# Fixed shares of other work behind the steps of each attention block, in place of a weaver that looks at readiness

## The chip, the cores and the metric

The kernel runs on one core of a Trainium2 chip. The metric is the device time of one execution in microseconds (us), the median of three runs. The kernel before takes 1716.58 us (1715.23 to 1721.32).

## What is computed

One layer of a hybrid block on 1024 positions of width 1024 in float32: a normalisation, one wide projection, an mLSTM branch in two directions (4 heads), a differential attention branch (8 heads), two gated output projections that are added, a last projection and a normalisation. The change touches only the attention:

```python
def diff_attention(q, k, v, lam):            # 8 heads, blocks of 128 queries
    def one_block(qb):
        scores = jnp.einsum('bqhjd,bkhjd->bhjqk', qb, k) * scale      # j = 2 halves of a head
        p = jax.nn.softmax(scores, axis=-1)
        p_diff = p[:, :, 0] - lam * p[:, :, 1]
        return jnp.einsum('bhqk,bkhd->bqhd', p_diff, v)
```

Queries and keys pass through a rotation by position (rope) first; the result of a head is normalised over its 128 columns and multiplied by a gate.

## The kernel before

Every float32 product is made of three matmuls on operands split into a high and a low part (`wH`, `wL`, `pH`, `pL`, and so on). The program is a list of units, each with a planned cost, and TensorE executes them in exactly the order of that list. The orders of the other engines come from a scheduler that puts each instruction where its own estimate of time finds it ready; at run time each engine then goes through its order strictly.

The attention has 8 heads of 8 blocks (t = 0 to 7, 128 queries each). `da_cycle` gives the units of one block:

- S: 12 matmuls into two PSUM tiles of two banks each. Behind it stand, off TensorE, per half a maximum on VectorE (line 963) and an exp on ScalarE (line 965), then three VectorE steps that give `e` = p0 - lam p1 (lines 969 to 971).
- T0 and T1: 4 transpositions each of the `e` of the block before, into one bank; then the casts `pH` (ScalarE, line 984) and `pL` (VectorE, line 985).
- P, in odd blocks: 24 matmuls (line 996) with the values of two earlier blocks; behind them a ScalarE copy `att` (line 998).
- M, in even blocks: 2 transpositions of `att` and two squares on ScalarE (line 1008), which write in the same bank. After the fourth M of a head (block 2 of the next head) eight small GpSimd steps (lines 145 to 151 and 1015) make a root.
- G, in blocks 4 and 5: 4 transpositions, and a VectorE step `zg` (line 1028) that reads them.

T, P, M and G share two PSUM banks (tag T): each of them needs a bank that an earlier one has given back. For T0 and T1 this is a bank of P (given back by the `att` copy), of M (by its second square) or of G (by the `zg` step); which of them is settled when the program is built.

Between these units stands other work, in pieces of three matmuls of 512 columns (line 460) or, for the values, six of 256 columns (line 482). In even heads these are the rope projection of the next head (pieces 1 to 32) and its gate z (33 to 48); in odd heads the rope projection (1 to 32) and the values of the next two heads (33 to 64); in the last head 32 pieces of gates for a later stage. The rope projection hands on a chain: two VectorE products from PSUM (lines 894 and 895), GpSimd `m` (896, 897), ScalarE casts `hl` (899), GpSimd remainders (900), DMAs to `kst` and `qq`. Its weights are cast on ScalarE (`wH`, line 193) and completed on GpSimd (`wL`, line 194).

The order of units and pieces is the work of `Weaver.weave`: it takes next the unit whose inputs and banks its plan holds to be ready soonest, and among equals the one that lies furthest behind in its share of the head. `z[h]` of odd heads are two loads without TensorE cost.

Of the kernel before, what the change touches and what calls it, by code (L numbers as in the profile page):

```python
# [13 lines left out]

S = 1024
D = 1024
# [3 lines left out]
L = 256  # L20
NC = S // L
NB = L // 128
# [6 lines left out]
def two_pi_parts():  # L29
# [9 lines left out]
MM = 0.214  # L39
TP = 0.109  # L40

LAG = dict(Th=2.2, Sh=5.0, PVh=3.7, Mh=8.1, qk=14.0, T=6.8, PV=3.7, M=4.5, F=6.0, TTh=1.9, TT=3.2, POh=1.6,
           PO=1.7, Wh=0.3, W=2.0, STh=2.1, ST=4.9, th=1.8, t=4.1, aq=9.0, outh=6.6, out=14.0, G=6.0)
# [18 lines left out]
class Weaver:  # L62
# [28 lines left out]
    def weave(self, *lists):  # L91


        lanes = {}
        for i, un in enumerate(lists):
            total, c = sum(u.cost for u in un) or 1.0, 0.0
            for u in un:
                lanes.setdefault((i, u.lane), []).append((c / total, u))
                c += u.cost
        self.coming = {u.name for un in lists for u in un if u.name}  # L100
        heads = list(lanes.values())
        while heads:
            best = min(heads, key=lambda l: (max(self.ready(l[0][1]), self.now), l[0][0]))
            u = best.pop(0)[1]
            self.put(u)
            self.coming.discard(u.name)
            heads = [l for l in heads if l]


class Block:  # L110
# [199 lines left out]
    def big(self, n, dt=F32):  # L310
        return self.s0.tile([128, S + 4], dt, name=n, tag="big", bufs=6)

# [61 lines left out]
    def conv_sink(self, seg, n):  # L374
# [3 lines left out]
        def sink(i, j, ps, rest):  # L378
            if i not in box:
                box[i] = (self.big("cin"), [])  # L380
                p.memset(box[i][0][:, 0:2], 0.0)
                p.memset(box[i][0][:, S + 2:S + 4], 0.0)
            raw, got = box[i]
# [9 lines left out]
            w = lambda j: self.conv[:, j * 16 + base:j * 16 + base + 1]  # L393
            y = self.big("y")[:, 0:S]
            for half in range(2):
# [247 lines left out]
    def angles(self, an):  # L643
# [38 lines left out]
        for src in (cs, sn):  # L682
            reps.append(self.big("rep")[:, 0:S].rearrange("p (k a b) -> p k a b", k=8, a=4))
            for k in (0, 4):
# [258 lines left out]
    def da_parts(self, h, st):  # L943
        v, a, p, q, w1 = self.v, self.a, self.p, self.q, self.w1

        def scores(t):
            if t == 0:
                st["Z"] = w1.tile([128, 2, 8], F32, name="Z", tag="Z", bufs=2)
                st["ms"] = w1.tile([128, 8], F32, name="ms", tag="ms", bufs=2)
                st["att"] = w1.tile([128, S], F32, name="att", tag="att", bufs=1)  # L950
            qq, k = st["q", t // 4], st["k"]
            c = slice((t % 4) * 128, (t % 4) * 128 + 128)
            Z = st["Z"]
            both = [self.bank("S", (128, S)) for _ in range(2)]

            for o in (slice(0, 512), slice(512, S)):
                for m, (x, y) in enumerate(((0, 0), (0, 1), (1, 0))):
                    for j, ps in enumerate(both):
                        r = slice(64 * j, 64 * j + 64)
                        self.t.matmul(ps[:, o], lhsT=qq[r, x, c], rhs=k[r, y, o], start=(m == 0), stop=(m == 2))  # L960
            for j, ps in enumerate(both):
                nm = w1.tile([128, 1], F32, name="nm", tag="nm", bufs=3)
                v.tensor_reduce(out=nm, in_=ps, axis=AX.X, op=ALU.max, negate=True)  # L963
                e = w1.tile([128, S], F32, name=f"e{j}", tag=f"e{j}", bufs=2 if j == 0 else 1)
                a.activation(out=e, in_=ps, func=AF.Exp, bias=nm[:, 0:1], accum_out=Z[:, j, t:t + 1])  # L965
                st["e", j] = e
            e0 = st["e", 0]
            r = w1.tile([128, 1], F32, name="r", tag="r", bufs=1)
            v.reciprocal(out=r, in_=Z[:, 1, t:t + 1])
            v.tensor_scalar(out=r, in0=r, scalar1=Z[:, 0, t:t + 1], scalar2=self.nlam[:, 0:1], op0=ALU.mult, op1=ALU.mult)  # L970
            v.scalar_tensor_tensor(out=e0, in0=e, scalar=r[:, 0:1], in1=e0, op0=ALU.mult, op1=ALU.add)
            st["p", t] = e0

        def transposes(t, g):
            pt = st["p", t]
            s = slice((t % 2) * 128, (t % 2) * 128 + 128)
            if t % 2 == 0:
                st["pT", t // 2, g] = (w1.tile([128, 4, 256], F32R, name="pH", tag="pH", bufs=2),
                                       w1.tile([128, 4, 256], F32R, name="pL", tag="pL", bufs=2))
            pH, pL = st["pT", t // 2, g]  # L980
            ps = self.bank("T", (128, 4, 128))
            for i in range(4):
                self.tr(ps[:, i, :], pt[:, (4 * g + i) * 128:(4 * g + i + 1) * 128])
            a.copy(pH[:, :, s], ps)  # L984
            v.tensor_tensor(out=pL[:, :, s], in0=ps, in1=pH[:, :, s].bitcast(F32), op=ALU.subtract)  # L985
# [14 lines left out]
        def squares(t2):  # L1000
            pt = self.bank("T")
            for i in range(2):
                t = 2 * t2 + i
                self.tr(pt[:, i * 128:(i + 1) * 128], st["att"][:, t * 128:(t + 1) * 128])
            for i in range(2):
                t = 2 * t2 + i
                x = pt[:, i * 128:(i + 1) * 128]
                a.activation(out=x, in_=x, func=AF.Square, accum_out=st["ms"][:, t:t + 1])
            if t2 == 3:
                zz = w1.tile([128, 8], F32, name="zz", tag="zz", bufs=1)  # L1010
                Z0 = st["Z"][:, 0, :]
                p.tensor_scalar(out=zz, in0=Z0, scalar1=EPS, scalar2=None, op0=ALU.mult)
                p.tensor_tensor(out=zz, in0=zz, in1=Z0, op=ALU.mult)
                rs = self.rsqrt(w1, st["ms"], 1.0 / 128.0, zz, "rb", eng=p)
                p.tensor_scalar(out=rs, in0=rs, scalar1=(1.0 - LAMBDA_INIT) * 0.5, scalar2=None, op0=ALU.mult)
                for half in range(2):
                    g = st["g", half]
                    p.tensor_tensor(out=g, in0=st["att"][:, half * 512:(half + 1) * 512], in1=g, op=ALU.mult)
                st["rs"] = rs

        def scale(half):
# [3 lines left out]
            for i in range(4):  # L1025
# [3 lines left out]
            q.dma_start(out=self.yb[h][:, half * 512:(half + 1) * 512], in_=g)  # L1029

        return dict(
            S=lambda t: Unit(6 * MM, lambda: scores(t), tag="S", hold=LAG["Sh"], name=("S", h, t), after=((("qk", h), LAG["qk"]),)),
            T=lambda t, g: Unit(4 * TP, lambda: transposes(t, g), tag="T", hold=LAG["Th"], name=("T", h, t, g),
                                after=((("S", h, t), LAG["T"]),)),
            PV=lambda t2, g: Unit(12 * TP, lambda: pv(t2, g), tag="T" if g == 0 else None, hold=LAG["PVh"], name=("PV", h, t2, g),
                                  after=((("T", h, 2 * t2 + 1, g), LAG["PV"]),)),
            M=lambda t2: Unit(2 * TP, lambda: squares(t2), tag="T", hold=LAG["Mh"], name=("M", h, t2),
                              after=((("PV", h, t2, 1), LAG["M"]), (("z", h if t2 == 3 else -1), 0.0))),
            G=lambda half: Unit(4 * TP, lambda: scale(half), tag="T", hold=LAG["Th"], name=("G", h, half),
                                after=((("M", h, 3), LAG["F"]),)))  # L1040
# [425 lines left out]
    def build(self):  # L1466
# [21 lines left out]
        with pool(name="const", bufs=1) as self.const, \  # L1488
# [22 lines left out]
            for n in range(NH_A):  # L1511
# [5 lines left out]
                if n < 3:  # L1517
                    blocks = (("gb", 4), ("gb", 5)) if n == 0 else (("bz", 4 * n - 3), ("bz", 4 * n - 1))
# [26 lines left out]
            w = Weaver()  # L1545
            w.add(enter("h", "hpool"), enter("tab", "tab", side="right"), enter("tf", "tf", side="right"),
                  enter("p0", "p0", side="right"), banks("ps0", T=6), keep(E.PE, E.Activation, E.DVE, E.Pool), do(begin))
            k = self.PIECES
# [30 lines left out]
            for i, x in enumerate(products + [None]):  # L1579
                y = products[i - 1] if i else None  # L1580
                un = sum(([x[0]] if x else []) + ([y[6]] if y else []) + ([x[3]] if x else []) + ([y[5]] if y else [])
                         + ([x[1], x[4], x[2]] if x else []), [])
# [5 lines left out]
            qk, z = zip(*[self.da_proj(h, sts[h]) for h in range(NH_B)])  # L1588
            w.add(do(lambda: setattr(self, "ahead", True)), *qk[0], *self.da_v(0, sts[0:2]))
            prev = None  # L1590
            for h in range(NH_B):
                cur = self.da_parts(h, sts[h])
                main = sum((self.da_cycle(cur, prev, t) for t in range(8)), [])
                ahead = qk[h + 1] if h + 1 < NH_B else []
                if h + 1 == NH_B:
                    nxt = fill(FILL[h])
                elif h % 2 == 1:
                    nxt = ahead + self.da_v((h + 1) // 2, sts[h + 1:h + 3])
                else:
                    nxt = ahead + z[h]  # L1600
                if h % 2 == 1:

                    k = [i for i, u in enumerate(main) if u.name and u.name[0] == "G"][-1] + 1
                    main[k:k] = z[h]
                w.weave(main, nxt)
                prev = cur
            end = sum((self.da_cycle(None, prev, t) for t in range(6)), [])
            w.weave(end[:-2], fill(2))
# [25 lines left out]
            k = len(passA) // 2  # L1634
# [52 lines left out]
```

## Time and profile before

| | |
|---|---|
| median of three runs | 1716.58 us |
| the profiled execution | 1714.09 us, span 1712.3 us |
| TensorE busy in the span | 1651.9 us (96%) |
| ScalarE, VectorE, GpSimd busy | 789.2, 1003.2, 630.7 us |
| granted TensorE clock, mean | 0.994 of full speed |
| attention, about 499 to 1105 us of the span | 606 us |

Busy time of TensorE is modelled, since matmuls overlap: a matmul of 256 columns is shown as 0.28 us long while the next one starts 0.12 us later. In the timeline the distance from start to start is therefore the price of an instruction, and an idle stretch costs somewhat more than its idle time.

### The profile page before, as it was taken

The numbers are of one execution on the slowest core, as the hardware profiler recorded it, in microseconds if no ns is written. First come the engines' busy times: TensorE is split into PE (matmuls) and PEld (weight loads), VectorE is DVE, ScalarE is ACT, GpSimd is POOL, SyncE is SP. The second block draws the span as 40 slices with busy tenths as digits, with TensorE's granted clock in tenths as the row PEclk, the third lists the DMA queues.
The fourth block names the chain that finished last, engine by engine and source line by source line (L and its number), as shares of the span: only waits on it lengthen the run. The fifth ranks groups of instructions, "written<-read, shape, count | busy, mean of one in ns | idle before, by whom it ended". The sixth has DMA issues, their size and how long they took to land. (4 is left out here: it accounts for less than half of the span.)

```text
span 1712.3 us, 25475 instructions
## 1 busy us (share of the span) xinstructions
PE 1651.9 (96%) x9395; PEld 1384.6 (81%) x9395; DVE 1003.2 (59%) x1817; ACT 789.2 (46%) x1578; POOL 630.7 (37%) x698
## 2 busy tenths in 40 slices
PE   7999999999999999999999999999999989999998
PEld 5777877888787897788779778789999877888887
DVE  5778586666538666766666566425666743235533
ACT  7455454544435554545454455324655644122221
POOL 5767566666534323241433332122321411222000
PEclk9999999999999999999999999999999999999999
DMA  5344343443443212222312131165454327344222
GB/s 183 94 128 128 107 129 117 135 148 111 124 99 75 49 51 62 74 69 56 83 33 70 50 87 50 56 184 164 140 167 155 93 85 254 122 147 136 87 88 85
DMA packets 177935, 182.99 MB, mean 107 GB/s; under 512 B 12441, under 2 KB 135666, under 8 KB 177810
## 3 DMA queue, kind: packets, MB, share of 16 engines
q1 hardware_dynamic: 176898, 179.78, 35.1%
q8 instruction: 74, 1.21, 0.3%
q10 hardware_dynamic: 912, 1.59, 0.2%
q14 instruction: 51, 0.42, 0.1%
HBM read 116.21 MB, written 48.33 MB: 96 GB/s over the span
## 5 line engine op out<-in xcount | busy, mean ns | idle before, releaser
L460 PE MATMUL pj<-hH,wH 128*128 128x512 f32 x544 | 227.7, 419 | 1.9 <-ACT f L573 1.5
L460 PE MATMUL pj<-hH,wL 128*128 128x512 f32 x544 | 214.3, 394 | 1.8 <-POOL wL L207 1.8
L460 PE MATMUL pj<-hL,wH 128*128 128x512 f32 x544 | 213.4, 392 | 0.2 <-DVE hL L611 0.2
L965 ACT ACTIVATE e<-S,nm 128x1024 f32<-128x1024 f32 x128 | 142.4, 1114 | 75.2 <-DVE nm L963 74.5
L209 POOL TENSOR_TENSOR wL<-raw,wH 128x1024 fp32r<-128x1024 f32 x35 | 85.2, 2434 | 235.8 <-ACT wH L204 231.1
L963 DVE TENSOR_REDUCE nm<-S 128x1 f32<-128x1024 f32 x128 | 150.5, 1217 | 9.6 <-PE S L960 9.0
L482 PE MATMUL pj<-wH,hH 128*128 128x256 f32 x512 | 149.9, 293 | 0.3
L482 PE MATMUL pj<-wL,hH 128*128 128x256 f32 x512 | 144.8, 283 | 1.4 <-POOL wL L207 1.4
L482 PE MATMUL pj<-wH,hL 128*128 128x256 f32 x512 | 144.5, 282 | 0.0
L985 DVE TENSOR_TENSOR pL<-T,pH 128x512 fp32r<-128x512 f32 x128 | 86.9, 687 | 87.9 <-ACT pH L984 86.4
L460 PEld LDWEIGHTS pj<-hH,wH 128*128 128x128 f32 x544 | 102.8, 189 | 32.2 <-issue 13.8
L460 PE MATMUL pj<-sl_yb,wH 128*128 128x512 f32 x384 | 120.8, 394 | 4.3 <-ACT sl_yb L1351 2.1
L460 PEld LDWEIGHTS pj<-hH,wL 128*128 128x128 f32 x544 | 102.4, 188 | 26.3 <-POOL wL L207 3.4
L460 PEld LDWEIGHTS pj<-hL,wH 128*128 128x128 f32 x544 | 103.1, 189 | 15.8 <-DVE hL L611 0.6
L960 PE MATMUL S<-kst,qq 64*128 64x512 f32 x768 | 108.3, 412 | 1.7 <-ACT e L965 1.7
L204 ACT CAST wH<-raw 128x1024 fp32r<-128x1024 f32 x50 | 52.5, 1050 | 123.4 <-PE pj L460 103.6
L291 PE MATMUL T<-TH,wL 128*128 128x512 f32 x304 | 102.5, 398 | 2.9 <-ACT u L298 2.2
L291 PE MATMUL T<-TH,wH 128*128 128x512 f32 x304 | 102.8, 398 | 0.0
L482 PEld LDWEIGHTS pj<-wH,hH 128*128 128x128 f32 x512 | 97.7, 191 | 5.4 <-issue 2.2
L984 ACT CAST pH<-T 128x512 fp32r<-128x512 f32 x128 | 75.1, 586 | 58.0 <-PE T L131 56.2
L482 PEld LDWEIGHTS pj<-wL,hH 128*128 128x128 f32 x512 | 97.5, 190 | 2.3 <-POOL wL L207 2.3
L482 PEld LDWEIGHTS pj<-wH,hL 128*128 128x128 f32 x512 | 97.7, 191 | 0.1
(367 smaller groups left out, 4260.9 us busy)
## 6 DMA issues: line engine op xcount, KB each, us to landing
raw<-in_w_in_dram SPq DMA_DIRECT2D x88, 512.0 KB, 4.3
kst<-hl SPq DMA_DIRECT2D x64, 128.0 KB, 2.4
qq<-hl SPq DMA_DIRECT2D x64, 128.0 KB, 2.4
x<-in_x_dram SPq DMA_DIRECT2D x8, 512.0 KB, 7.3
cak<-y SPq DMA_DIRECT2D x16, 256.0 KB, 2.3
cakH<-cin SPq DMA_DIRECT2D x16, 256.0 KB, 2.5
cakL<-tz SPq DMA_DIRECT2D x16, 256.0 KB, 2.2
gm<-oz SPq DMA_DIRECT2D x16, 256.0 KB, 3.2
```

Of the source, the lines that this page charges most:

```text
L204: self.a.copy(wH, raw)
L209: self.p.tensor_tensor(out=wL, in0=raw, in1=wHf, op=ALU.subtract)
L291: self.t.matmul(ps, lhsT=l[:, k, :], rhs=r[:, k, :], start=(first and k == 0 and m == 0), stop=(k == 3 and m == 2), skip_group_check=not f ...
L460: self.t.matmul(ps, lhsT=l[:, k, :], rhs=r, start=(n == 0), stop=(n == 23))
L482: self.t.matmul(ps[:, i, :], lhsT=l, rhs=r[:, k, :], start=(kh == 0 and k == 0 and m == 0), stop=(kh == 1 and k == 3 and m == 2))
L960: self.t.matmul(ps[:, o], lhsT=qq[r, x, c], rhs=k[r, y, o], start=(m == 0), stop=(m == 2))
L963: v.tensor_reduce(out=nm, in_=ps, axis=AX.X, op=ALU.max, negate=True)
L965: a.activation(out=e, in_=ps, func=AF.Exp, bias=nm[:, 0:1], accum_out=Z[:, j, t:t + 1])
L984: a.copy(pH[:, :, s], ps)
L985: v.tensor_tensor(out=pL[:, :, s], in0=ps, in1=pH[:, :, s].bitcast(F32), op=ALU.subtract)
```

## The change

A new method `Weaver.blocks` replaces `weave` in the heads of the attention. It gives each block of a head the same planned length (units and other work together) and puts the other work behind the units of the block in fixed shares: 2 behind S, 3 behind M, 0.5 behind G, nothing between the two halves of P, 1.5 behind P, 2.5 behind T0 and 3.5 behind T1. It no longer asks whether a unit is planned to be ready. The planned cost of S goes from 6 to 8 matmuls. The loads z of odd heads keep their place behind G in block 5. The end of the attention after the last head is woven as before.

```diff
+    SHARE = {"S": 2.0, "M": 3.0, "G": 0.5, "PV0": 0.0, "PV1": 1.5, "T0": 2.5, "T1": 3.5}
+
+    def blocks(self, blocks, other):
+
+        other = list(other)
+        length = (sum(u.cost for un in blocks for u in un) + sum(u.cost for u in other)) / len(blocks)
+        done = 0.0
+        for n, un in enumerate(blocks):
+            share = [self.SHARE.get(u.name[0] + (str(u.name[3]) if len(u.name) > 3 else ""), 0.0) if u.name else 0.0 for u in un]
+            main = sum(u.cost for u in un)
+            room, given = (n + 1) * length - done - main, 0.0
+            for k, u in enumerate(un):
+                self.put(u)
+                upto = room * sum(share[:k + 1]) / sum(share)
+                while other and given + other[0].cost / 2 <= upto:
+                    given += other[0].cost
+                    self.put(other.pop(0))
+            done += main + given
+        self.add(*other)
...
-            S=lambda t: Unit(6 * MM, lambda: scores(t), ...
+            S=lambda t: Unit(8 * MM, lambda: scores(t), ...
...
-                main = sum((self.da_cycle(cur, prev, t) for t in range(8)), [])
+                main = [self.da_cycle(cur, prev, t) for t in range(8)]
...
-                    k = [i for i, u in enumerate(main) if u.name and u.name[0] == "G"][-1] + 1
-                    main[k:k] = z[h]
-                w.weave(main, nxt)
+                    k = [u.name and u.name[0] for u in main[5]].index("G") + 1
+                    main[5][k:k] = z[h]
+                w.blocks(main, nxt)
```

The first place is TensorE in block 4 of an odd head (here head 1). `rb_y` marks G, `e0` marks T0, `pj` is a piece of the values. Before, T0 stands behind four pieces and takes the bank of G, which VectorE gives back:

```order
L482 MATMUL pj_5557<-wH_5430,hL0_176 128x256
L482 MATMUL pj_5557<-wL_5431,hH0_174 128x256
L131 MATMUL T_5612<-ident_150,e0_5413 128x128 [waits DVE_49]
L131 MATMUL T_5612<-ident_150,e0_5413 128x128 x3
L482 MATMUL pj_5557<-wH_5430,hH0_174 128x256
```

In the changed program T0 follows G directly and waits for ScalarE:

```order
L504 MATMUL pj_5531<-wL_5147,hH0_174 128x256
L153 MATMUL T_5593<-ident_150,rb_y_5356 128x128 [waits DVE_49]
L153 MATMUL T_5593<-ident_150,rb_y_5356 128x128 x3
L153 MATMUL T_5600<-ident_150,e0_5436 128x128 [waits Activation_49]
L153 MATMUL T_5600<-ident_150,e0_5436 128x128 x3
L504 MATMUL pj_5531<-wH_5146,hH0_174 128x256
```

What moved: the pieces between G and T0 are gone, and T0 now takes the bank of M, which the second square gives back.

The second place is ScalarE around the same block, from the end of block 3. `hl` is the rope chain, `e0` and `e1` are the exps of block 4, `T_5576` are the squares of its M. Before:

```order
L899 CAST hl_5506<-m1_5427 128x512
L965 ACTIVATE e0_5539,Z_5117<-S_5523,nm_5537 128x1024
L965 ACTIVATE e1_5543,Z_5117<-S_5524,nm_5541 128x1024
L1008 ACTIVATE T_5576,ms_5118<-T_5576 128x128 x2
L984 CAST pH_5481<-T_5612 128x4x128
```

In the changed program:

```order
L215 CAST wH_5523<-raw_5408 128x8x64
L215 CAST wH_5523<-raw_5527 128x8x64
L921 CAST hl_5506<-m0_5400 128x512
L921 CAST hl_5506<-m1_5401 128x512
L987 ACTIVATE e0_5554,Z_5117<-S_5538,nm_5552 128x1024
L1030 ACTIVATE T_5576,ms_5118<-T_5576 128x128
L987 ACTIVATE e1_5558,Z_5117<-S_5539,nm_5556 128x1024
L1030 ACTIVATE T_5576,ms_5118<-T_5576 128x128
L1006 CAST pH_5478<-T_5600 128x4x128
L1006 CAST pH_5493<-T_5619 128x4x128
```

What moved: the two squares stand one behind each exp instead of behind both; the casts `wH` and `hl` stand ahead of the exps in both programs.

The third place is ScalarE from block 4 to block 5 of an even head (here head 2). Before:

```order
L899 CAST hl_6439<-m0_6347 128x512
L984 CAST pH_6363<-T_6474 128x4x128
L899 CAST hl_6439<-m1_6348 128x512
L965 ACTIVATE e0_6497,Z_6003<-S_6481,nm_6495 128x1024
L965 ACTIVATE e1_6501,Z_6003<-S_6482,nm_6499 128x1024
L998 COPY att_6005<-T_6517 128x256
```

In the changed program:

```order
L1006 CAST pH_6344<-T_6432 128x4x128
L215 CAST wH_6489<-raw_6036 128x8x64
L215 CAST wH_6489<-raw_6364 128x8x64
L921 CAST hl_6446<-m0_6356 128x512
L921 CAST hl_6446<-m1_6357 128x512
L987 ACTIVATE e0_6479,Z_6003<-S_6463,nm_6477 128x1024
L987 ACTIVATE e1_6483,Z_6003<-S_6464,nm_6481 128x1024
L1020 COPY att_6005<-T_6508 128x256
```

What moved: `pH` of T1 came between the two `hl` casts and now stands ahead of the weight casts; the `hl` casts and behind them the exps and `att` of block 5 come after.

## Rows read from the trace of the kernel before

**Rows 1.** The page, parts 1 and 5: engines' busy time, groups of instructions.

```profile
PE 1651.9 (96%) x9395; PEld 1384.6 (81%) x9395; DVE 1003.2 (59%) x1817; ACT 789.2 (46%) x1578; POOL 630.7 (37%) x698
...
L965 ACT ACTIVATE e<-S,nm 128x1024 f32<-128x1024 f32 x128 | 142.4, 1114 | 75.2 <-DVE nm L963 74.5
...
L963 DVE TENSOR_REDUCE nm<-S 128x1 f32<-128x1024 f32 x128 | 150.5, 1217 | 9.6 <-PE S L960 9.0
```

**Rows 2.** Busy time by stretch (PE, PEld, DVE, ACT, POOL), clock, DMA: heads 1, 2, attention.

```profile
562.00:642.00 80.00, 79.37 (x561) 68.81 (x560) 51.61 (x74) 39.90 (x86) 25.45 (x26) 1.00 0.21 53
642.00:716.00 74.00, 69.56 (x424) 55.13 (x424) 49.91 (x70) 39.28 (x83) 29.84 (x27) 1.00 0.28 73
...
sum 606.00, PE 588.20 PEld 485.51 DVE 401.13 ACT 309.63 POOL 197.10; mean PE 73.53 PEld 60.69 DVE 50.14 ACT 38.70 POOL 24.64
```

**Rows 3.** Timeline of TensorE, undisturbed: start, length, operation; P, T, pieces, S, M.

```profile
1051.67 0.28 PE L996 MATMUL T<-pH,vH 128*128 128x256 f32 x1
...
1054.50 0.60 PE L131 MATMUL T<-ident,e 128*128 128x128 f32 x4
1054.85 0.48 PE L460 MATMUL pj<-hH,wH 128*128 128x512 f32 x1
...
1057.71 0.60 PE L131 MATMUL T<-ident,e 128*128 128x128 f32 x4
1058.24 1.65 PE L960 MATMUL S<-kst,qq 64*128 64x512 f32 x12
1059.83 0.44 PE L131 MATMUL T<-ident,att 128*128 128x128 f32 x2
```

**Rows 4.** Timeline of TensorE: four of its waits, idle time and releaser in brackets.

```profile
651.00 0.66 PE L131 MATMUL T<-ident,e 128*128 128x128 f32 x4 [1.39 <-ACT T L1008]
...
674.21 0.39 PE L996 MATMUL T<-pH,vH 128*128 128x256 f32 x1 [1.28 <-ACT pH L984]
...
714.88 0.66 PE L131 MATMUL T<-ident,e 128*128 128x128 f32 x4 [0.59 <-ACT att L998]
...
1002.10 0.58 PE L996 MATMUL T<-pH,vH 128*128 128x256 f32 x1 [2.35 <-DVE pL L985]
```

**Rows 5.** Short stretches around waits; the number before the last two is the clock.

```profile
824.00:828.00 4.00, 2.38 (x18) 1.98 (x17) 1.44 (x2) 1.72 (x3) 3.85 (x4) 0.97 0.02 6
828.00:832.00 4.00, 4.00 (x18) 3.52 (x18) 2.60 (x5) 3.01 (x6) 0.00 (x0) 0.60 0.89 203
...
983.00:987.00 4.00, 4.00 (x24) 3.18 (x24) 2.60 (x5) 3.90 (x8) 0.31 (x1) 1.00 0.89 204
...
1374.00:1377.00 3.00, 3.00 (x11) 2.53 (x10) 0.42 (x1) 0.78 (x3) 0.23 (x1) 0.50 0.50 169
```

**Rows 6.** Timeline of TensorE at the start of block 4 of head 1.

```profile
601.82 1.66 PE L960 MATMUL S<-kst,qq 64*128 64x512 f32 x12
603.41 0.38 PE L482 MATMUL pj<-wH,hH 128*128 128x256 f32 x1
...
605.67 0.38 PE L131 MATMUL T<-ident,att 128*128 128x128 f32 x2
```

**Rows 7.** The same stretch on ScalarE and GpSimd.

```profile
601.77 1.15 ACT L193 CAST wH<-raw 128x512 fp32r<-128x512 f32 x2
...
607.53 0.62 ACT L899 CAST hl<-m 128x512 fp32r<-128x512 f32 x1 [0.63 <-POOL m L897]
608.06 1.11 ACT L965 ACTIVATE e<-S,nm 128x1024 f32<-128x1024 f32 x1
...
602.47 2.54 POOL L194 TENSOR_TENSOR wL<-raw,wH 128x512 fp32r<-128x512 f32 x2 [6.26 <-ACT wH L193]
604.96 1.29 POOL L896 TENSOR_TENSOR m<-m,hl 128x512 f32<-128x512 f32 x1
```

**Rows 8.** Timeline of ScalarE at the start of heads 2 and 4.

```profile
650.55 0.28 ACT L1008 ACTIVATE T<-T 128x128 f32<-128x128 f32 x1
...
798.99 1.05 ACT L204 CAST wH<-raw 128x1024 fp32r<-128x1024 f32 x1 [2.33 <-DMA raw<-in_w_in_dram]
```

More of the change, by code (lines that the diff above doesn't have):

```diff
@@ L1031, in da_parts @@
         return dict(
-            S=lambda t: Unit(6 * MM, lambda: scores(t), tag="S", hold=LAG["Sh"], name=("S", h, t), after=((("qk", h), LAG["qk"]),)),
+            S=lambda t: Unit(8 * MM, lambda: scores(t), tag="S", hold=LAG["Sh"], name=("S", h, t), after=((("qk", h), LAG["qk"]),)),
             T=lambda t, g: Unit(4 * TP, lambda: transposes(t, g), tag="T", hold=LAG["Th"], name=("T", h, t, g),
```

## The prediction

> **What bounds the kernel now.** I read the page first: TensorE is busy for 1651.9 us of the span [rows 1], no other engine for more than 59%. So only TensorE's own time and its waits count. Then the busy time by stretch, one head at a time: the attention takes 606.00 us, with TensorE busy for 588.20 [rows 2], so 17.8 us are idle. Head 1 loses 0.6 of its 80 us, head 2 loses 4.4 of its 74 [rows 2]; the other odd and even heads repeat these two.
>
> The third view is the timeline of TensorE, start to start. Undisturbed, 24 matmuls of P take 2.83 us, T 0.35 (0.53 in front of S), four pieces behind a T 2.86 (about 0.78 for the first, 0.69 for each further one), S 1.59 [rows 3], a piece of the values 0.71 [rows 6]. With these prices I laid out all 64 blocks. 45 come out within 0.1 us of the trace; the others exceed it, and the excess sums to 29 us: 0.4 in head 0, 0.8 in each odd head (squares), 20 in heads 2, 4 and 6 together, 6.6 at the end of the last head, where the pieces run out. It is more than the idle time because the array refills after a wait, and because the clock falls behind some waits. The kinds are seen in [rows 4]: T waits for the squares (1.39), P for `pH` (1.28), T for `att` (0.59), P for `pL` (2.35). The clock: one wait of head 4 (1.6 us idle in 4) is followed by 4 us at a mean of 0.60, the same wait in head 6 by none at 1.00, and a wait of 2.9 us in the mLSTM stage by 3 us at 0.50 [rows 5]: the lower of the two levels, for some 3 us, worth about 1.5 us each.
>
> **What the change removes.** No matmul is added or taken away; switches between kinds of work cost 0.1 to 0.17 each and their number stays within a few, so I set that at 0 (between -1 and +1). The longest possible gain is thus the 29 us. Gone by the new order: the odd heads' wait for the squares (the second square now stands ahead of `pH`), the `att` wait of block 7 (two pieces now stand between T0 and T1), the `pL` wait at P in block 5 (`pH` no longer stands between the `hl` casts), most of the waits at the end of the last head (its 32 pieces now last to block 7), and the 0.4 of head 0.
>
> **What it puts in their place.** The planner no longer looks at readiness, so I looked for every T, P, M and S at what it waits for in the changed order, and timed it by the chain of ScalarE.
>
> *The chain.* In head 1 the `wH` casts start at 601.77, as soon as the last rope piece has let the weights go. GpSimd begins `wL` 0.70 later, `m` 3.19 later, the second `hl` cast stands at 5.76, and only then comes the exp of block 4, 6.29 us after `wH` [rows 7], although S began at 601.82 [rows 6]. Before, nothing on TensorE asked for that exp soon: four pieces stand between G and T0, eight between M and T1. They were the cover.
>
> *A, block 4 of heads 1, 3, 5.* The last rope piece now ends 0.8 us ahead of block 4, so `wH` starts at -0.66 (block 4 at 0) and the exp at 5.63. Then square, exp, square: an exp is 1.11 [rows 1], a square about 0.27 [rows 8], so the second square starts at 8.13, and TensorE goes on 0.45 later (650.55 [rows 8] to 651.00 [rows 4]): 8.58. T0, which now needs the bank of M, is due after S 1.59, two pieces 1.53, M 0.14, two pieces 1.51 and G 0.36: 5.13. The wait is 3.45, three times 10.3 us.
>
> *B, block 5 of heads 2, 4, 6.* The last rope piece closes block 4, so `wH` starts at 0.04, the exp at 6.33, the second exp and `att` follow at 7.5 and 8.6, and T1, which needs the bank of P, can start about 0.45 after that (as after a square), at 9.05. It is due after S, a piece, G, P, T0 and one piece: 6.74. The wait is 2.3, three times 6.9.
>
> *F, block 5 of head 0.* The same chain, with `wL`, `m`, `wL`, remainder, `m` on GpSimd: exp at 5.7, `att` at 8.0, T1 8.45 against 6.35: 2.1.
>
> *C, block 0 of heads 2, 4, 6.* A weight cast that waits 2.33 for its DMA [rows 8] stands ahead of the exps in both programs. The second square comes 1.2 earlier than before, T1 1.4 earlier: the excess of 0.6 (1.6 in head 2) becomes 0.8 (1.8): 3.4.
>
> *D, block 3 of heads 2, 4, 6.* The first rope `m` now stands ahead of the root's eight steps, so the wait of P (1.28 and more [rows 4], an excess of 2.15) falls to about 0.2; the maxima behind the same `pL` on VectorE, and through them `att` for T1, remain 0.7 late: 0.9 each (between 0 and 2.15), 2.7.
>
> *E and G, T0 directly behind G.* The second square is free at 4.65 (maximum 1.22, exp 1.11 [rows 1] behind S). T0 is due at 4.36 in even heads, 3.66 in the last: 0.3 three times and 1.0. With 0.3 for `att` in the last head's short blocks: 2.2.
>
> These sum to 10.3 + 6.9 + 2.1 + 3.4 + 2.7 + 2.2 = 27.6 us, so without the clock the balance is -29 + 27.6 = -1.4.
>
> *The clock.* The 29 us contain about 4 of half clock. The new waits are fewer and longer: six of A and B, one of F, one of C are at or above 1.8 us. The nearest rows are the two at 0.60 and 0.50 [rows 5] and the one without a fall. At none of the eight it is 0, at all of them 8 times 1.5 = 12; I take 7, since the wait of 2.9 did fall and A is longer still.
>
> The sum is -1.4 + 7 = +5.6. Against its own profiled execution of 1714.09 us that makes 1719.7; the median lies 2.5 above that execution, so I forecast 1722 us.
>
> **The rivals.** *Slower: the clock takes more.* If the clock falls behind all eight long waits and twice over behind A, because TensorE comes out of a 3.4 us wait into short runs broken by the next T, that is 11 times 1.5 = 16.5 in place of 7, and 1716.6 - 1.4 + 16.5 gives 1732. It decides if the clock behind A stays at the lower level for more than 4 us. For it: the row at 0.50. Against it: head 2 waits several times and shows 1.00 over its length [rows 2]. The Trainium skill (Perfetto Trace Analysis, section Matmul Optimizations) says that the matmul engine scales its power with utilization and that matmuls should go back to back in batches; the change halves the runs of pieces. By that rule alone all heads would lose clock, whatever the waits; head 1, whose runs are already broken up, keeps 1.00 [rows 2], so the trace doesn't bear it out for runs without waits.
>
> *Faster: the cover is not needed.* If A doesn't come, because the weight casts and `hl` leave ScalarE earlier than the chain says, 10.3 and half of the clock go: 1722.2 - 10.3 - 3.5 = 1708. If B doesn't either, 6.9 and the rest of the clock go: 1698. For it: the orders were laid out by a scheduler that expected these exps in time. Against it: the same chain of casts is in the trace with 6.29 us, and nothing in it changes but its place.
>
> *The change doesn't do what it says: the waits stay.* Two banks for T, P, M and G are few, and the waits may only change places without a balance: 1716 to 1717. The Trainium skill (Perfetto Trace Analysis, section Optimization Strategy) takes consistent bubbles as a sign that there may not be enough PSUM for the next tile. Two of the four kinds in [rows 4] are waits for a bank, two are for data; so the rule covers half of what I see.
>
> **How the numbers follow.** The forecast, 1716 to 1725, has 0.55, of which I count all as within 0.5%; about 0.5% (8.6 us, so 1708.0 to 1725.2) is what a measurement of this kernel can tell from no change. The slower rival, 1726 to 1736, has 0.29, the faster one, 1690 to 1708, has 0.11, waits that only move 0.05. So faster 0.11, same 0.60, slower 0.29. The unknown terms (switches by 1 either way, D by 3, the clock by 7 down and 5 up) give 1711 to 1729 around the forecast; to leave out no more than 2 in 10, the range reaches into both rivals: 1705 to 1732.
>
> **What would show it.** In the trace of the changed kernel T in block 4 of heads 1, 3 and 5 should wait about 3.3 us for the squares, and T in block 5 of heads 2, 4 and 6 about 2.2 us for `att`; the waits of P for `pH` and `pL` should be nearly gone; the last head should hold its pieces to block 7 and lose about 1.3 in place of 6.6. The attention should take about 611 us in place of 606. It is wrong if the waits in A or B are under 1 us (then 1700 to 1710), or if waits stand at S or at P that I haven't listed (then above 1728).

## The result, and the profile after

The changed kernel takes 1723.34 us (median of 15 runs, 1721.05 to 1727.23) against 1718.36 us of the kernel before (15 runs beside them, 1715.23 to 1721.32). The ratio is 1.0036, with a 95% interval of 1.0027 to 1.0045: some 5 us slower, clearly apart from zero, yet inside the half per cent that was called no change. The forecast was 1722.

The page of the changed kernel, parts 1 and 5, answers to [rows 1]:

```profile
PE 1653.1 (96%) x9395; PEld 1381.5 (80%) x9395; DVE 1006.7 (58%) x1817; ACT 787.7 (46%) x1578; POOL 626.6 (36%) x698
...
L987 ACT ACTIVATE e<-S,nm 128x1024 f32<-128x1024 f32 x128 | 142.2, 1111 | 118.7 <-DVE nm L985 118.7
L985 DVE TENSOR_REDUCE nm<-S 128x1 f32<-128x1024 f32 x128 | 150.5, 1217 | 26.2 <-PE S L982 26.1
...
L153 PE MATMUL T<-ident,e 128*128 128x128 f32 x512 | 78.4, 277 | 22.8 <-ACT T L1030 11.8
```

TensorE does the same work (1653.1 us busy against 1651.9). The exps' idle time has grown from 75.2 to 118.7 us, but most of it lies off the path: the long waits of TensorE below (A, B and F) don't come by way of it. The line to read is the last: 22.8 us stand in front of the transposes of `e`. The waits of TensorE in the attention, kernel before (engine, line, whom it waited for; total us, times, longest):

```profile
PE T L996 <- DVE pL L985: 5.0, 6, 2.4
PE T L131 <- ACT T L1008: 4.1, 6, 1.4
PE T L996 <- ACT pH L984: 3.8, 3, 1.3
PE T L131 <- ACT att L998: 2.0, 4, 0.6
PE S L960 <- ACT e L965: 1.7, 2, 1.1
PE T L131 <- DVE pL L985: 0.9, 2, 0.8
```

and the changed kernel:

```profile
PE T L153 <- ACT T L1030: 11.8, 7, 3.1
PE T L153 <- ACT att L1020: 10.9, 8, 2.9
PE T L1018 <- DVE pL L1007: 1.0, 3, 0.3
```

Six kinds of short wait have become two kinds of long wait and a small rest; both are of T for a PSUM bank that ScalarE still has to read. One by one, on the timeline of TensorE of the changed kernel:

```profile
549.53 0.66 PE L153 MATMUL T<-ident,e 128*128 128x128 f32 x4 [2.86 <-ACT att L1020]
...
614.94 0.66 PE L153 MATMUL T<-ident,e 128*128 128x128 f32 x4 [3.07 <-ACT T L1030]
...
685.69 0.66 PE L153 MATMUL T<-ident,e 128*128 128x128 f32 x4 [0.42 <-ACT att L1020]
...
704.90 0.66 PE L153 MATMUL T<-ident,e 128*128 128x128 f32 x4 [1.83 <-ACT att L1020]
```

In order: block 5 of head 0 (term F), block 4 of head 1 (A, again with 3.06 and 3.07 in heads 3 and 5), block 3 of head 2 (D, also in heads 4 and 6), block 5 of head 2 (B, then 1.82 and 2.08).

To see what each block loses I again set the start-to-start time of all 64 blocks against the prices of [rows 3]; "excess" below is that difference. It sums to 29.3 us before and 34.7 after: +5.4. The attention, from the first S to the first values of the mLSTM stage, grew from 626.1 to 631.7 us: +5.6. The two profiled spans differ by more (1712.3 and 1721.4). The other 3.5 us lie in stages whose order the change doesn't touch, 3.0 of them behind the attention, and the medians don't show them.

### The profile page after: what moved, and what is told of

The parts are those of the page before. It is cut to its first block, busy times and chain, and to the rows that moved or that the text cites. A ratio compares the mean times of both kernels' runs of the same rounds, so it can differ in the third digit from the quotient of the medians.

```text
span 1721.4 us, 25487 instructions
## 1 busy us (share of the span) xinstructions
PE 1653.1 (96%) x9395; PEld 1381.5 (80%) x9395; DVE 1006.7 (58%) x1817; ACT 787.7 (46%) x1578; POOL 626.6 (36%) x698
## 5 line engine op out<-in xcount | busy, mean ns | idle before, releaser
L482 PE MATMUL pj<-hH,wH 128*128 128x512 f32 x544 | 231.5, 426 | 1.9 <-ACT f L595 1.5
L987 ACT ACTIVATE e<-S,nm 128x1024 f32<-128x1024 f32 x128 | 142.2, 1111 | 118.7 <-DVE nm L985 118.7
L153 PE MATMUL T<-ident,e 128*128 128x128 f32 x512 | 78.4, 277 | 22.8 <-ACT T L1030 11.8
```

The costliest lines, as they stand in the source:

```text
L153: self.t.transpose(out, in_, self.ident[0:k, 0:k])
L482: self.t.matmul(ps, lhsT=l[:, k, :], rhs=r, start=(n == 0), stop=(n == 23))
```

## The experiments

First comes the cause, taken away and made worse; then how far each block's loss reaches; then the way out. One question needed no run: with S planned at 6 again, as before the change, the fixed shares give the same order on all five engines; the new planned cost of S has no part in the result.

**The cast that stands in the way.** The one edit, in the changed kernel and in the kernel before:

```diff
-                a.copy(hl[:, i, :], m[i])
+                p.tensor_copy(out=hl[:, i, :], in_=m[i])
```

Changed kernel with it:

> Changed kernel with one edit: the rope's casts to hl run on GpSimd instead of ScalarE, so that no cast that waits for GpSimd's product stands ahead of an exp on ScalarE; TensorE's order is as in the changed kernel. Theory (fixed shares cover too little of a lateness that comes from this in-order cast): the waits of block 4 of heads 1, 3, 5 (3.07 each), of block 5 of heads 2, 4, 6 (1.82 to 2.08 each), of block 5 of head 0 (2.86) and half of those of block 3 go, with the clock behind two of them (3.1): 1723.3 - 9.2 - 5.7 - 2.9 - 2 - 3.1 = about 1700. Rival 1 (two PSUM banks for transposes are too few whatever ScalarE does, or the clock reacts to short runs alone): the waits stay, 1721 to 1725. Rival 2 (GpSimd, now longer busy, becomes the late one): waits of the score products of the next head on the roped queries and keys, 1725 or more.

Kernel before with it:

> Kernel before with the same single edit (hl cast on GpSimd). Theory: in the kernel before the same cast cost the even heads their waits of PV in blocks 3 and 5 (5.0 and 3.8 in the table of waits) and the transposes' 4.1, about 12 of the 29 us of excess, so about 1706; the changed kernel with this edit is then as fast or faster. Rival (the weaver's waits come from its order, not from the cast): 1717 to 1719.

Measured: 1700.81 us (ratio to the kernel before 0.9911, 0.9897 to 0.9924) and 1703.73 (0.9930, 0.9917 to 0.9942). What goes on in block 4 of head 1 is seen on ScalarE, first in the changed kernel (the block starts at 606.50):

```profile
605.75 1.14 ACT L215 CAST wH<-raw 128x512 fp32r<-128x512 f32 x2
610.26 0.62 ACT L921 CAST hl<-m 128x512 fp32r<-128x512 f32 x1 [3.37 <-POOL m L918]
611.50 0.62 ACT L921 CAST hl<-m 128x512 fp32r<-128x512 f32 x1 [0.63 <-POOL m L919]
612.03 1.11 ACT L987 ACTIVATE e<-S,nm 128x1024 f32<-128x1024 f32 x1
...
614.50 0.27 ACT L1030 ACTIVATE T<-T 128x128 f32<-128x128 f32 x1
```

and then with the cast on GpSimd (the block starts at 607.03):

```profile
606.27 1.14 ACT L215 CAST wH<-raw 128x512 fp32r<-128x512 f32 x2
609.98 1.12 ACT L987 ACTIVATE e<-S,nm 128x1024 f32<-128x1024 f32 x1 [2.57 <-DVE nm L985]
...
612.46 0.27 ACT L1030 ACTIVATE T<-T 128x128 f32<-128x128 f32 x1
```

The exp starts 2.95 into the block in place of 5.53, now held by the maxima alone, and T waits 0.50 us where it waited 3.07:

```profile
612.89 0.66 PE L153 MATMUL T<-ident,e 128*128 128x128 f32 x4 [0.50 <-ACT T L1030]
```

ScalarE was not busy in between: the line of the `hl` casts in the attention of the changed kernel shows an engine that stands idle at the head of its queue for 58.5 us (53.5 before):

```profile
L921 ACT CAST hl<-m 128x512 fp32r<-128x512 f32 x28 | 17.4, 621 | 58.5 <-POOL m L918 37.9 <-POOL m L919 20.6
```

The excess falls from 34.7 to 8.9, with TensorE's order the same instruction for instruction. A, B, D, F and a wait in block 3 of head 0 shrink or go together, so one cause is behind all of them, and neither the two banks nor the short runs are it. C keeps its 2.6. In the kernel before the excess falls from 29.3 to some 13: the waits of P in blocks 3 and 5 and of T for the squares in the odd heads are gone, and what is left is mostly at the end of the last head (7). Part of the gain was lost at the start, as the second rival had it: head 0's rope lies open, and its first S came at 504.06 in place of 499.92.

**The same cause, made worse.** One more GpSimd step ahead of `m`:

```diff
+            idle = w1.tile([128, 512], F32, name="idle", tag="idle", bufs=1)
+            p.tensor_tensor(out=idle, in0=m[0], in1=fb(hl[:, 2]), op=ALU.subtract)
             p.tensor_tensor(out=m[0], in0=m[0], in1=fb(hl[:, 2]), op=ALU.subtract)
```

> Changed kernel plus one more step on GpSimd of about 1.28 us ahead of each rope's sum m, into a tile that nobody reads: the chain wL, m, hl is later by that much, TensorE's and ScalarE's orders are unchanged. Theory: each wait that hangs on hl grows by about 1.3 (three in block 4 of heads 1, 3, 5, three in block 5 of heads 2, 4, 6, some in blocks 3 and in head 0): 6 to 9 times 1.3, so 1731 to 1735. Rival (the lateness is ScalarE's own queue of exps, casts and copies, not the cast that waits for GpSimd): 1722 to 1725.

Measured: 1748.23 us (1.0185, 1.0170 to 1.0201). The waits did what the theory said; the same places as above, and their like in head 4:

```profile
555.90 0.72 PE L153 MATMUL T<-ident,e 128*128 128x128 f32 x4 [4.22 <-ACT att L1022]
...
625.24 1.12 PE L153 MATMUL T<-ident,e 128*128 128x128 f32 x4 [4.41 <-ACT T L1032]
...
715.58 0.66 PE L153 MATMUL T<-ident,e 128*128 128x128 f32 x4 [3.05 <-ACT att L1022]
...
877.93 1.11 PE L153 MATMUL T<-ident,e 128*128 128x128 f32 x4 [3.04 <-ACT att L1022]
```

F grew by 1.36, A by 1.34, B by 1.22: the GpSimd step (1.29 in the trace of head 1, 1.37 until the next one starts) lies on the path one to one, 9.1 us over the seven. The total was missed, and upward: the attention began 3.5 later, new waits (0.86 to 0.88 in block 2 of heads 1, 3, 5, 1.06 in head 0) brought 5, and behind the seven longer waits some 11 us more were lost to the clock. These 11 are not measured one by one: they are what is left of the 24 us of growth from the first S to block 4 of the last head, once 1.5 is added back that block 3 of heads 2, 4 and 6 lost less. The edit was not quite pure: the scheduler also let the second `m` go ahead of the root's longest step there, and turned round the two `hl` casts of block 5 of heads 2, 4 and 6. After 3.04 us of waiting in head 4 the granted clock was at its lower level for the next 4 us, and the stretch behind it was mixed (the third number from the right is the clock):

```profile
878.00:882.00 4.00, 4.00 (x12) 2.96 (x14) 2.61 (x4) 0.95 (x2) 0.00 (x0) 0.50 0.78 179
882.00:886.00 4.00, 4.00 (x21) 2.78 (x20) 1.64 (x2) 0.52 (x3) 0.00 (x0) 0.75 0.55 149
```

**Cover in front of one transpose.** The cast left alone, other shares in block 4 only (four pieces, or three, between G and T0):

```diff
-            share = [self.SHARE.get(u.name[0] + ...
+            table = dict(self.SHARE, G=6.0, T0=2.0, T1=0.0) if n == 4 else self.SHARE
+            share = [table.get(u.name[0] + ...
```

> Changed kernel with another share table in block 4 alone: G 6.0, T0 2.0, T1 0, so that the first transpose of block 4 stands four pieces (odd heads) or three (even heads) behind G instead of none; no other block and no other engine's work changes. Theory (the cover in front of the transpose decides): the waits in block 4 of heads 1, 3, 5 (4.93, 4.93, 3.38 with the clock) go, with 0.35 in each even head and 1.0 in the last: 1723.3 - 13.2 - 2 = about 1708 to 1711; the waits in blocks 3 and 5 stay. Rival 1 (waits only move: block 5 becomes later by what block 4 gains): 1720 to 1724. Rival 2 (the clock falls with the four pieces gone from the end of the block): 1716 or more.

Measured: 1708.10 us (0.9954, 0.9942 to 0.9967). The wait of block 4 fell to 0.19 in head 1, and those of block 5 stayed in the main (1.41 in place of 1.83 in head 2):

```profile
614.20 0.66 PE L154 MATMUL T<-ident,e 128*128 128x128 f32 x4 [0.19 <-ACT T L1031]
...
699.17 0.66 PE L154 MATMUL T<-ident,e 128*128 128x128 f32 x4 [1.41 <-ACT att L1021]
```

Excess 34.7 to 19.3, and nothing was handed on to block 5. One line of the table made the change faster than the kernel before.

**The change by head.** The weaver's order in heads 0, 1, 3, 5, the fixed shares in heads 2, 4, 6, 7 (S planned at 6, so that each head is in its order row for row):

```diff
-                w.blocks(main, nxt)
+                if h in (2, 4, 6, 7):
+                    w.blocks(main, nxt)
+                else:
+                    w.weave(sum(main, []), nxt)
```

> The change by head: heads 0, 1, 3, 5 in the weaver's order, row for row as before, heads 2, 4, 6 and 7 in the fixed shares, row for row as after; all casts on ScalarE. Theory (the loss is a sum of local waits, each of its own block): heads 2, 4, 6 wait 15.2 with the shares where they waited 19.6 with the weaver, head 7 1.3 where it was 6.5, and the losses of head 0 (4.0) and of heads 1, 3, 5 (10.9) don't come: 1718.4 - 4.4 - 5.2 = about 1709. Rival (a head's waits depend on the order of the head before it, lateness is handed on): 1714 to 1720.

Measured: 1707.15 us (0.9947, 0.9933 to 0.9962). Heads 2, 4, 6 have an excess of 15.4 (15.2 expected), head 7 of 1.3, heads 0, 1, 3, 5 of 2.7. That the even heads come so close is in part luck. Their blocks 3 and 4 repeat the changed kernel to 0.1, but C depends on the head before: it is 1.3 in place of 2.6. And behind the same wait in block 5 of head 6 the clock now fell, which cost some 1.6 (the third number from the right is the granted clock; first the run by head, then the changed kernel after its wait of 2.08):

```profile
1000.76 0.66 PE L153 MATMUL T<-ident,e 128*128 128x128 f32 x4 [2.11 <-ACT att L1020]
1002.00:1006.00 4.00, 4.00 (x17) 2.50 (x16) 1.51 (x4) 0.09 (x1) 0.00 (x0) 0.57 0.88 207
...
1017.00:1021.00 4.00, 3.84 (x23) 2.76 (x24) 2.96 (x6) 1.18 (x3) 0.00 (x0) 1.00 0.82 189
```

So the losses of A, B and D are local and add up by head, while C varies with the head before. The change won 4.4 us in the even heads and 5 in the last one, and lost 11 in heads 1, 3, 5 and 4 in head 0. Of the 4.4 some 3 are clock that the profiled execution of the kernel before lost in heads 4 and 6 (granted clock 0.60 from 828 to 832 us, [rows 5], and 0.59 from 1002 to 1006 us), and of the 11 some 3 are clock lost in heads 1 and 3.

**The way out.** The cast on GpSimd from head 1 on, head 0 as it was, in both programs; and, in the changed one, the shares of block 4 as above and one piece more ahead of T0 in block 0 as well:

```diff
-                a.copy(hl[:, i, :], m[i])
+                (a.copy if h == 0 else p.tensor_copy)(hl[:, i, :], m[i])
```

```diff
+    BY_BLOCK = {0: dict(M=4.5, T1=2.0), 4: dict(G=6.0, T0=2.0, T1=0.0)}
...
+            table = dict(self.SHARE, **self.BY_BLOCK.get(n, {}))
```

Changed kernel, cast moved from head 1 on:

> Changed kernel with the hl casts on GpSimd in heads 1 to 7 only; head 0 keeps them on ScalarE. In the version with all casts moved the attention began 4.1 later (504.06 against 499.92), since head 0's rope lies open ahead of the first scores. Theory: that start comes back and nothing else changes in heads 1 to 7, so 1700.8 - 4.1 = about 1697; head 0's waits in blocks 3 and 5 go too, since the casts that stood ahead of its exps are head 1's. Rival (the late start was something else, or what starts earlier waits later): 1700 to 1702.

With the shares of the two blocks too:

> The same, with two shares of its own for two blocks: block 4 G 6.0, T0 2.0, T1 0 (four pieces, or three, ahead of its first transposes), block 0 M 4.5, T1 2.0 (one piece more ahead of its first transposes). What the version with all casts moved still waits: 0.8 in block 4 of heads 1, 3, 5, 0.85 in block 0 of heads 2, 4, 6, 0.32 in block 4 of heads 2, 4, 6 and 1.0 in block 4 of the last: 6.9. Theory: most of it goes, 1697 - 5 = about 1692. Rival (each share added ahead of one transpose is missing at the next, waits only move): 1696 to 1698.

Kernel before, cast moved from head 1 on:

> Kernel before with the hl casts on GpSimd in heads 1 to 7 only. Theory: its attention, too, begins earlier again than with all casts moved (first block of head 0 then 2.6 later): 1703.7 - 3 = about 1700 to 1701, so that the two orders, each with the cast out of the way, differ by about 3 in favour of the fixed shares, where they differ by 5 in favour of the weaver with the cast in the way. Rival (the order costs the same 5 with and without the cast): about 1692, faster than the changed kernel with the same casts.

Measured: 1696.34 us (0.9880, 0.9863 to 0.9896), 1690.33 (0.9849, 0.9829 to 0.9868) and 1700.92 (0.9904, 0.9889 to 0.9919). The first S is back at 500.02. With the cast out of the way the fixed shares are 4.6 us faster than the weaver (their runs don't overlap: 1695.14 to 1697.20 against 1699.30 to 1701.29); with the cast in the way they were 5.0 slower. In heads 0 to 6 the weaver loses some 6 and the shares some 7; in blocks 5 to 7 of the last head, where the weaver has run out of pieces, it loses some 7 and the shares 0.1. In the version with both edits hardly anything is left: the attention on TensorE (window; PE busy first) and its waits,

```profile
495.00:1105.00 610.00, 609.39 (x3941) 505.25 (x3940) 415.19 (x555) 301.46 (x633) 231.07 (x241) 1.00 0.25 68
```

```profile
PE T L155 <- ACT att L1022: 0.5, 2, 0.4
```

That version, 1690.33 us, beats both kernels.

## Why the prediction was right, step by step

**The chain behind A.** In block 4 of head 1 the exp was to start 5.63 into the block, the second square 8.13, T at 8.58. It was 5.53, 8.00 and 8.44. Moving the cast, slowing the chain and adding cover each changed the wait as the chain says, so this is shown, not argued.

**What was to go.** It went: the excess of block 2 of heads 1, 3 and 5 fell from 0.8 to under 0.1, that of block 7 of heads 2, 4 and 6 from 0.8 to under 0.1, the 0.4 in block 1 of head 0 to nothing, that of the last head from 6.5 to 1.3.

**The terms**, in us of excess, clock apart:

| term | predicted | measured |
|---|---|---|
| A, block 4 of heads 1, 3, 5 | 10.3 | 10.1 |
| B, block 5 of heads 2, 4, 6 | 6.9 | 6.6 |
| F, block 5 of head 0 | 2.1 | 3.1 |
| C, block 0 of heads 2, 4, 6 | 3.4 | 2.6 |
| D, block 3 of heads 2, 4, 6 | 2.7 | 4.9 |
| E, G, the last head's 0.3 | 2.2 | 2.3 |
| block 3 of head 0 | not listed | 1.3 |
| clock | 7 | 3.1 |
| blocks under 0.2 | none | 0.7 |
| sum | 34.6 | 34.7 |

The sum agrees better than its parts, so its closeness is in part luck: the clock was 3.9 too dear and C 0.8, and F, D, head 0 and the small ones 5 too cheap.

**What was mis-sized.** *D*: the first rope `m` did get ahead of the root's steps, as said, but the second still stands behind three of them, of which one takes 2.55 (676.13 to 678.68 on GpSimd), and behind its `hl` the second `pH` and so P and the maxima. ScalarE of the changed kernel in block 3 of head 2:

```profile
679.98 0.62 ACT L921 CAST hl<-m 128x512 fp32r<-128x512 f32 x1 [3.76 <-POOL m L919]
680.50 0.58 ACT L1006 CAST pH<-T 128x512 fp32r<-128x512 f32 x1
```

P stops twice for it and T1 once (0.42 above), 1.65 in each head in place of 0.9; the given bound of 2.15 held. *Head 0, block 3*: I looked at each block for its own waits and not for lateness from the block before. The `hl` casts of block 2 held the exps there by 4.01 us, and the combination and maxima of block 3 were late in turn (0.94 at T1, 1.30 in all). *F*: one GpSimd step of the chain took 2.28 in place of 1.28 (below). *C*: head 2 lost 0.82 like heads 4 and 6, not 1.8; what cost it one more before did not carry over, and why is open. The piece added in block 0 cleared C, all but 0.3 to 0.6 that came up in block 1.

**The clock.** Of the seven long waits that came two were followed by the lower level, worth 1.55 each (block 4 of heads 1 and 3 exceeds 4.93, that of head 5 3.38, for the same wait). The 7 us were chosen between none and all, and the result lies in the lower half. The 3.1 are what one execution lost, and no fixed price: see the last section.

**The rivals.** That the waits only move fell with the order by head: they changed place and sum. That the cover is not needed fell with the waits themselves. The runs of pieces were not halved, either: some 420 pieces stood in 190 unbroken stretches and now stand in 236. That the clock takes more didn't come at 3.07 us of waiting; at 4.41 it did, where each of the three A's was followed by the lower level.

## What to carry to other kernels

When an order that looks at readiness gives way to fixed shares, go through the in-order queues of the other engines and look for the step that waits at their head: what it holds up must be covered in every block, and a table of shares covers the average block only. An engine busy for 46% can set the time through one 0.6 us cast that waits for a slower engine, and moving that cast was worth 27 us (ratio 1.0036 to 0.9880), five times the difference between the two orders, and turned its sign. Sum the excess by block and head before judging a reordering: here it won in half of the heads and lost in the others.

## What the runs showed of the hardware

The clock after equal waits is not the same. Behind block 4 of heads 1, 3 and 5 of the changed kernel, after 3.07, 3.06 and 3.07 us of idle TensorE and the same work before and after (the third number from the right is the granted clock):

```profile
614.00:618.00 4.00, 3.06 (x19) 3.06 (x20) 2.32 (x4) 1.47 (x5) 0.00 (x0) 0.77 0.86 199
618.00:622.00 4.00, 4.00 (x29) 3.74 (x29) 1.54 (x3) 1.33 (x3) 0.00 (x0) 0.81 0.46 130
771.00:775.00 4.00, 3.32 (x21) 3.32 (x22) 2.32 (x4) 1.21 (x5) 0.00 (x0) 0.77 0.88 202
775.00:779.00 4.00, 4.00 (x29) 3.69 (x29) 1.54 (x3) 1.33 (x3) 0.00 (x0) 0.81 0.38 110
927.00:931.00 4.00, 2.58 (x22) 2.59 (x23) 2.32 (x4) 1.97 (x6) 0.40 (x1) 1.00 0.77 178
931.00:935.00 4.00, 4.00 (x33) 3.33 (x32) 1.74 (x4) 1.31 (x3) 0.00 (x0) 1.00 0.55 150
```

Twice the level fell from 2.4 to 1.2 GHz for some 3 us, once it didn't. What decides it stays open, and it isn't the length of the wait alone: the wait of 2.11 us in the run by head was followed by a fall, that of 2.86 us in block 5 of head 0 of the changed kernel by none (granted clock 1.00 from 549 to 557 us). Nor does the length say when the fall comes. In the changed kernel TensorE is already at work again; in the kernel with the longer chain the first T is already slow after 4.41 us (1.12 in place of 0.66) and after 3.04 us (1.11), but hardly after 4.22 us (0.72) and not after 3.05 us (0.66), where the clock fell a little later (0.57 from 556 to 560 us and 0.60 from 716 to 720 us). It also differs between executions of one program: of the 15 of the changed kernel the two fastest (1721.05 and 1721.14 us) had a mean granted clock of 0.995, two of the slower ones (1725.87 and 1727.23 us) of 0.991. That spread of 6 us is larger than the distance between the two kernels' medians. The Trainium skill (TensorE: Matmul & The Clock Gate, section What's actually happening) says that the chip's look at activity is not aligned with the program, so that the point of change varies between runs. Two falls behind three equal waits, and executions that differ, fit that; no run here tests it.

VectorE and GpSimd wait for each other. In block 5 of head 0 the combination of `e` on VectorE takes 2.19 us; behind it a rope step on GpSimd takes 2.28. Undisturbed they take 1.28 and 1.29. GpSimd, then VectorE, of the changed kernel (the first line on GpSimd and the last on VectorE are undisturbed ones):

```profile
517.72 1.29 POOL L918 TENSOR_TENSOR m<-m,hl 128x512 f32<-128x512 f32 x1 [9.87 <-DVE hl L916]
...
539.11 1.28 POOL L216 TENSOR_TENSOR wL<-raw,wH 128x512 fp32r<-128x512 f32 x1 [11.27 <-ACT wH L215]
540.35 2.28 POOL L918 TENSOR_TENSOR m<-m,hl 128x512 f32<-128x512 f32 x1
```

```profile
539.27 2.19 DVE L993 SCALAR_TENSOR_TENSOR e<-e,r,e 128x1024 f32<-128x1024 f32 x1
...
685.91 1.28 DVE L993 SCALAR_TENSOR_TENSOR e<-e,r,e 128x1024 f32<-128x1024 f32 x1
```

VectorE starts while `wL` runs and ends 1.07 behind it; `m` starts while VectorE runs and ends 1.17 behind that. The rows read as taking turns, each step waiting out the other's. The Trainium skill (SBUF — State Buffer, section SBUF: two separate sides) says the same: the two share a pair of ports, and the one that starts first keeps it for its whole instruction, with a VectorE step of two SBUF inputs among those that need it. It is about the 1 us by which F was too small. With the casts on GpSimd from head 1 on the mean of this VectorE step went from 1418 to 1516 ns, which reads as more such meetings; the attention was faster all the same.
